# Layer 0's second projection in full fp32, attention ahead of the S5 products, and main products dealt by weight

## The chip, the cores and the metric

The kernel runs on one core of one Trainium2 chip. The metric is the device time of one execution in microseconds (us), the median of several runs. A core has a matrix engine (TensorE, PE in the profile, with its weight loads as PEld), a vector engine (VectorE, DVE), a scalar engine (ScalarE, ACT), a general one (GpSimd, POOL) and a queue that issues DMAs (SyncE, SP). Each engine works its own instructions in a fixed order, and waits for others by semaphores.

## The reference

Two layers of an encoder. Each layer normalizes its input, projects it, runs three mixers beside each other on parts of the projection (a gated linear recurrence with a convolution, an S5 state space model, sliding-window attention with rotary positions), projects their outputs back, and adds an MLP with squared ReLU:

```python
hn = _rms_norm(x, p['norm1'])
proj = hn @ p['w_in']
u_a, g_a, u_b = proj[..., :o1], proj[..., o1:o2], proj[..., o2:o3]
q = proj[..., o3:o4]; k = proj[..., o4:o5]; v = proj[..., o5:]
...
mix = jnp.concatenate([out_a, out_b, out_c], axis=-1) @ p['w_out']
x = x + mix
act = jnp.square(jax.nn.relu(_rms_norm(x, p['norm2']) @ p['w_up']))
x = x + act @ p['w_down']
```

The model width is 1024, the MLP's 4096, and there are 512 prompt and 128 sample frames. All inputs and outputs are fp32.

## The kernel before, in words

The 640 frames are cut into two groups g of 320 columns (256 prompt and 64 sample frames). Activations are kept transposed, with the width in 8 tiles of 128 partitions.

**Units and halves.** The work of PE is mostly weight products. A `Unit` is one block of 128 output columns over the 8 tiles of the width; it goes in two halves of 4 tiles each. A *split* unit has its weights cut in a high part wh (an ACT copy, L243) and a low part wl (a DVE subtraction, L244), activations likewise, and makes three products for each tile (L274, L275, L276). A *full* unit makes one fp32 product for each tile (L271) from weights as they come by DMA; the profile shows two records for each of these. Before the change only group 0 of layer 0's projection is full. `stream` is a generator that gives one half at a step and empties a unit's bank when it is done; there are three PSUM banks for units ("mm"), four for small products ("sm") and one for norms ("fin").

**Norm.** `Norm` scales the input by its gain only (L348 in a full one; L351 on ACT and L352 on DVE in a split one). The sum of squares goes through ACT, POOL and at last three one-column products on PE (L377); then eight small DVE operations (L396 to L403) make the reciprocal root, and PE spreads it over the partitions (L414). The result r scales what comes out of the banks. cs, the cosines and sines of the rotation times r, is scaled on POOL (L730). A k or q tile is copied by DVE as t = bank x cosine (L702 for k, L696 for q), by ACT as sw, which POOL multiplies by the sine (L693), and summed by DVE.

**Mixers.** `mixers` holds three generators: L (recurrence; its convolution is L760), S (S5: L832 makes the scans' inputs on PE, then scans on DVE, L850, with products on ACT, POOL and DVE, up to L855) and A (attention: loads, own keys, scores of the cached frames L963, probabilities, the transposes of their scaled scores L956 at L176, values L981, and then for each of 4 chunks of queries scores L1006, a turn by transposes with copies on ACT and DVE, L1020, and values L1027). The string TURNS says in which order they get a step. `weave` deals the halves of a stream evenly between the steps.

**Order.** PE's order is the code's order. On the other engines a scheduler decides it, with high priority for the emptying of full units' banks and for the norm. The S5 constants (`s5_const`) are made in the first 60 us by chains of complex products (L523 to L529), B's on DVE and C's on POOL, from values that DVE makes first (AR at L491); DVE makes other small constants in front of these (L439 to L518).

```python
    TURNS = "ALSSLSSSS" "LAAAAAA" + 5 * "SAA" + "A"
    ...
    weave(iter(()), 1, A, 15)
    weave(small, 2, A, 3)
    M = mixers(0, P, 0, q[0], m[0], setup[0])
    weave(M, 9, A, 4)
```

A is the stream of the projection, small the S5 constants' products, M the mixers.

## Time and profile before

| | before |
|---|---|
| runs, us | 1424.63, 1427.09, 1428.07 (median 1427.09) |
| profiled execution, us | 1423.95, span 1422.1 |
| TensorE's mean granted clock | 0.981 |
| PE, weight loads | 1358.9 us (96%), 1300.3 us (91%) |
| DVE, ACT, POOL | 876.0 us (62%), 651.7 us (46%), 359.4 us (25%) |

The profile is of one execution. Busy time is the time in which an engine worked on instructions; the rest of the span it waited or had nothing to do. The granted clock is 1.0 at 2.4 GHz and 0.5 at 1.2.

### The profile page before, as it was taken

What the parts mean: (1) busy time and instruction counts of PE and PEld (TensorE: products, weight loads), DVE (VectorE), ACT (ScalarE), POOL (GpSimd) and SP (SyncE); (2) the same over time, 40 slices, a digit from 0 to 9 for tenths busy, and PEclk for the clock granted to TensorE, in tenths of its full rate; (3) what the DMA queues carried; (4) which work ended last, traced back from release to release, by engine and by line L of the source; (5) the groups of instructions that cost most, each with busy time, mean ns of one, the idle gap of its engine ahead of it and who ended that gap; (6) DMA issues with size and microseconds to landing.
All of it is one profiled execution on the core that took longest, in us unless ns stands there. A gap on an engine that the chain in (4) does not pass through costs nothing.

```text
span 1422.1 us, 25428 instructions
## 1 busy us (share of the span) xinstructions
PE 1358.9 (96%) x9444; PEld 1300.3 (91%) x9444; DVE 876.0 (62%) x1726; ACT 651.7 (46%) x1347; POOL 359.4 (25%) x581
## 2 busy tenths in 40 slices
PE   7859979999999999999989998999999999999997
PEld 5648869899999999999988997999999999999997
DVE  7987696756554345356697769675654434435574
ACT  4365765545332132136675667554542212313543
POOL 5754364301042017001243325320101100100111
PEclk9979999999999999999999999999999999999998
DMA  7211332344422222234433332333442222223452
GB/s 261 81 61 63 116 104 101 125 151 145 151 72 78 74 75 63 81 120 149 143 99 112 120 126 83 112 112 126 142 149 89 75 75 75 75 75 117 151 177 91
DMA packets 91387, 156.24 MB, mean 110 GB/s; under 512 B 14336, under 2 KB 18304, under 8 KB 91264
## 3 DMA queue, kind: packets, MB, share of 16 engines
q1 hardware_dynamic: 91264, 154.63, 32.7%
q8 instruction: 74, 1.21, 0.3%
q14 instruction: 49, 0.40, 0.1%
HBM read 151.02 MB, written 3.37 MB: 109 GB/s over the span
## 4 chain that ended last, share of the span: by engine, by line
PE 82%; DVE 9%; POOL 4%; issue 2%; ACT 1%; DMA 0%; SPq 0%; DVEq 0%; ACTq 0%
PE mm L274 25%; PE mm L275 25%; PE mm L276 25%; PE sm L176 2%; DVE wl L244 1%; PE mm L271 1%; PE sm L1027 1%; DVE bigf L853 1%; DVE bigf L850 1%; PE sm L868 1%; PE fin L414 1%; PE sm L981 1%; PE sm L896 1%; PE sm L1006 1%; PE sm L832 0%
## 5 line engine op out<-in xcount | busy, mean ns | idle before, releaser
L274 PE MATMUL mm<-bigr,wh 128*128 128x320 f32 x2592 | 817.6, 315 | 2.1 <-POOL bigr L156 1.8
L276 PE MATMUL mm<-bigr,wl 128*128 128x320 f32 x2592 | 805.3, 311 | 12.7 <-DVE wl L244 12.7
L275 PE MATMUL mm<-bigr,wh 128*128 128x320 f32 x2592 | 804.7, 310 | 1.6 <-DVE bigr L1112 1.6
L243 ACT ACTIVATE wh<-raw 128x512 fp32r<-128x512 f32 x520 | 327.4, 631 | 504.9 <-PE mm L275 484.2
L274 PEld LDWEIGHTS mm<-bigr,wh 128*128 128x128 f32 x2592 | 490.2, 189 | 15.7 <-issue 5.8
L276 PEld LDWEIGHTS mm<-bigr,wl 128*128 128x128 f32 x2592 | 490.4, 189 | 14.0 <-DVE wl L244 14.0
L275 PEld LDWEIGHTS mm<-bigr,wh 128*128 128x128 f32 x2592 | 490.6, 189 | 3.0 <-DVE bigr L1112 2.1
L244 DVE TENSOR_TENSOR wl<-raw,wh 128x512 fp32r<-128x512 f32 x520 | 375.9, 724 | 181.2 <-ACT wh L243 169.5
L156 POOL TENSOR_SCALAR bigr<-t 128x320 fp32r<-128x320 f32 x128 | 63.3, 496 | 611.2 <-ACT t L1110 611.1
L1094 DVE TENSOR_TENSOR xT<-xT,mm 128x320 f32<-128x320 f32 x160 | 77.9, 487 | 135.4 <-PE mm L276 135.2
L1110 ACT ACTIVATE t<-t 128x320 f32<-128x320 f32 x128 | 60.0, 472 | 120.3 <-DVE t L1109 104.5
L1112 DVE TENSOR_TENSOR bigr<-t,bigr 128x320 fp32r<-128x320 f32 x128 | 71.0, 556 | 71.5 <-POOL bigr L156 71.2
L1109 DVE SCALAR_TENSOR_TENSOR t<-mm,r 128x320 f32<-128x320 f32 x128 | 62.1, 489 | 74.5 <-PE mm L276 73.7
L371 POOL TENSOR_TENSOR ss<-ss,sq 128x320 f32<-128x320 f32 x58 | 53.2, 918 | 201.4 <-ACT sq L364 194.6
L364 ACT ACTIVATE sq<-xT 128x320 f32<-128x320 f32 x66 | 30.6, 463 | 17.0 <-POOL ss L371 11.0
L271 PE MATMUL mm<-bigf,raw 128*128 128x320 f32 x104 | 31.8, 453 | 3.0 <-DVE t L702 2.4
L693 POOL TENSOR_TENSOR sw<-sw,cs 128x320 f32<-128x320 f32 x20 | 18.1, 905 | 58.2 <-ACT sw L692 44.4
L176 PE MATMUL sm<-ident,att 128*128 128x128 f32 x88 | 13.9, 289 | 19.7 <-DVE att L956 19.1
L956 POOL TENSOR_SCALAR att<-att,st 128x192 f32<-128x192 f32 (+2 forms) x24 | 22.6, 950 | 39.5 <-ACT wh L243 31.0
L351 ACT ACTIVATE bigr<-xT,sm 128x320 fp32r<-128x320 f32 x56 | 30.5, 560 | 2.7 <-DVE xT L1094 1.0
L271 PEld LDWEIGHTS mm<-bigf,raw 128*128 128x128 f32 x104 | 20.2, 199 | 11.9 <-DVE t L702 2.9
L352 DVE SCALAR_TENSOR_TENSOR bigr<-xT,sm,bigr 128x320 fp32r<-128x320 f32 x56 | 30.4, 551 | 0.1
(292 smaller groups left out, 1072.7 us busy)
## 6 DMA issues: line engine op xcount, KB each, us to landing
raw<-w_up SPq DMA_DIRECT2D x192, 256.0 KB, 2.6
raw<-w_down SPq DMA_DIRECT2D x192, 256.0 KB, 2.6
raw<-w_in SPq DMA_DIRECT2D x85, 256.0 KB, 2.6
raw<-w_out SPq DMA_DIRECT2D x64, 256.0 KB, 2.6
wl<-w_in SPq DMA_DIRECT2D x11, 256.0 KB, 4.0
xT<-x SPq DMA_DIRECT2D x8, 320.0 KB, 6.1
yT<-xT SPq DMA_DIRECT2D x8, 320.0 KB, 2.9
cs<-rope SPq DMA_DIRECT2D x4, 320.0 KB, 3.0
```

Source lines behind the costliest of these rows:

```text
L156: return G.tensor_scalar(out, in_, 1.0, 0.0, OP.mult, OP.add)
L243: act(h, raw, AF.Copy)
L244: tt(l, raw, h.bitcast(F32), OP.subtract)
L271: mm(pt, lhsT=self.w[n][:, k % 4], rhs=m[:, k], start=k == 0, stop=k == 7)
L274: mm(pt, lhsT=h[:, k % 4], rhs=m[:, k, 0], start=k == 0, stop=False)
L275: mm(pt, lhsT=h[:, k % 4], rhs=m[:, k, 1], start=False, stop=False)
L276: mm(pt, lhsT=l[:, k % 4], rhs=m[:, k, 0], start=False, stop=k == 7)
L371: G.tensor_tensor(self.ss, self.ss, sq, OP.add)
L1094: tt(xT[:, g, k], xT[:, g, k], pt, OP.add)
L1109: V.scalar_tensor_tensor(t, pt, 0.0, norm.r, OP.max, OP.mult)
L1110: act(t, t, AF.Square)
L1112: mark["dve"] = tt(am[:, f, 1], t, am[:, f, 0].bitcast(F32), OP.subtract)
```

## The change

Layer 0's projection is in full fp32 for group 1 as well, so its 24 halves take L271 on weights as loaded. In group 0 of layer 0 the squares of the norm are kept apart, and PE sums them in 24 one-column products (L395 of the new file) instead of POOL's additions and three products. That projection's units come in another order: k, v, q0 to q3, then ua, ub and ga. The first eight attention steps of this group come before the products of the S5 constants. `weave` gets a list of weights, one for each step: how many halves come behind it; TURNS holds both, with a list of its own for layer 0's group 0 (True). Projection, output projection and the first MLP piece are chained to one stream, so that the weights run over their borders. In the recurrence two copies of states move up, and one more step is cut. Tiles of the projection are allocated when first written.

```diff
-    def weave(steps, n, fill, m):
-
-        done = 0
-        for i in range(n):
+    def chain(*gens):
+        for g in gens:
+            yield from g
+
+    def later(f):
+        yield from f()
+
+    def weave(steps, weights, fill, m):
+
+        done, w, total = 0, 0, sum(weights)
+        for v in weights:
             next(steps, None)
-            while done < (i + 1) * m // n:
+            w += v
+            while done < int(w * m / total + 1e-6):
                 next(fill, None)
                 done += 1
...
             if full:
-                self.h = Carve(bigf()).at(0, 8, NG)
+                c = Carve(bigf())
+                self.h, self.sq = c.at(0, 8, NG), c.at(8 * NG, 8, NG)
...
-            if k == 0:
+            if self.full and self.g == 0:
+                act(self.sq[:, k], x, AF.Square)
+                if k == 0:
+                    V.tensor_scalar(self.sq[:, 0], self.sq[:, 0], 1e-6 * DM / 128, None, OP.add)
+                self.todo.append((self.sq[:, k], k == 0, k == 7))
+            elif k == 0:
...
+        order = (4, 5, 6, 7, 8, 9, 0, 1, 2, 3, 10, 11) if L == 0 and g == 0 else range(12)
...
-    TURNS = "ALSSLSSSS" "LAAAAAA" + 5 * "SAA" + "A"
+
+    TURNS = {False: "A0 L3 S1 S1 L1 S1 S1 L1 S2 S6 A1 A1 L6 A2 A1 A1 A1 A1 S2 A1 A1 S2 A1 A1 S3 A1 A1 S3 A1 A1 S2 A1 A1".split(),
+             True: "A1 A1 A1 A1 A1 A1 A1 A1 L4 A1 A1 L1 A1 S1 S1 L1 A1 A2 S1 S1 A1 A1 S2 S6 A1 L6 A1 A1 S2 S2 S2 S2 S2".split()}
+    WEIGHTS = {k: [int(t[1:]) for t in v] for k, v in TURNS.items()}
...
-        norms[g] = Norm(g, n1(0), full=g == 0)
+        norms[g] = Norm(g, n1(0), full=True)
...
-    weave(iter(()), 1, A, 2)
+    turns(A, 2)
     dma(sm[:, 80:], a["sm"][:, 80:])
     small_prep()
     s5_small(lru_const())
     small = layer_small(0, P)
     next(small)
     first(1)
-    weave(iter(()), 1, A, 15)
-    weave(small, 2, A, 3)
+    turns(A, 10)
     M = mixers(0, P, 0, q[0], m[0], setup[0])
-    weave(M, 9, A, 4)
-    run(A)
+    tw = WEIGHTS[True]
+    F = chain(A, stream(in_proj(0, 1, norms[1], q[1])))
+    weave(M, tw[0:9], F, 9)
+    run(small)
+    weave(M, tw[9:], F, 19)
+    tw = WEIGHTS[False]
     for L in range(DEPTH):
         last = L == DEPTH - 1
-        A = stream(in_proj(L, 1, norms[1], q[1]))
-        weave(M, 23 if L == 0 else 8, A, 16)
-        run(M)
+        if L:
+            F = stream(in_proj(L, 1, norms[1], q[1]))
+            turns(F, 10)
         M = mixers(L, P, 1, q[1], m[1])
-        weave(M, 9, A, 8)
-        run(A)
         hm = {}
-        F = stream(out_proj(L, 0, m[0], hm))
-        weave(M, 7, F, 16)
-        run(F)
-        F = stream(mlp(L, 0, (0,), hm, fresh=(0,)))
-        weave(M, 16, F, 28)
+        F = chain(F, stream(out_proj(L, 0, m[0], hm)), later(lambda: stream(mlp(L, 0, (0,), hm, fresh=(0,)))))
+        weave(M, tw, F, 58 if L else 52)
         run(M, F)
         run(stream(out_proj(L, 1, m[1], hm)))
...
-            A = stream(in_proj(L + 1, 0, norms[0], q[0]))
-            weave(iter(()), 1, A, 14)
+            F = stream(in_proj(L + 1, 0, norms[0], q[0]))
+            turns(F, 10)
             M = mixers(L + 1, P, 0, q[0], m[0])
-            weave(M, 9, A, 10)
-            run(A)
-            F = stream(mlp(L, 3, (1,), hm, nxt, norms))
-            weave(M, 15, F, 32)
-            run(F)
+            F = chain(F, stream(mlp(L, 3, (1,), hm, nxt, norms)))
+            weave(M, tw, F, 46)
+            run(M, F)
```

Three places show how instructions move. The first is PE's start, before and now, from the first unit on (L271 is a product of a full unit with weights in tiles raw or wl; L377 and L395 sum squares, L414 and L432 spread r, t is v's tile).

```order
L271 MATMUL mm<-bigf,raw 128x320 x12
L377 MATMUL fin<-ones,ss 128x1 x3
L271 MATMUL mm<-bigf,wl 128x320 x4
L271 MATMUL mm<-bigf,raw 128x320 x4
L414 MATMUL fin<-ident,rsq 128x128 x2
L414 MATMUL fin<-ident,rsq 128x64
L271 MATMUL mm<-bigf,wl 128x320 x4
L271 MATMUL mm<-bigf,raw 128x320 x4
```

```order
L271 MATMUL mm<-bigf,raw 128x320 x12
L395 MATMUL fin<-ones,bigf 128x1 x24
L271 MATMUL mm<-bigf,wl 128x320 x4
L271 MATMUL mm<-bigf,raw 128x320 x4
L432 MATMUL fin<-ident,rsq 128x128 x2
L432 MATMUL fin<-ident,rsq 128x64
L271 MATMUL mm<-bigf,wl 128x320 x4
L271 MATMUL mm<-bigf,raw 128x320 x4
L176 MATMUL sm<-ident,t 128x128 x2
```

Before, r is followed by units that are ua, ub and k; now the 12 and 8 products ahead of it and the one half behind it are k, v and q0, and the next is q1's.

The second is POOL's queue from group 1's squares (ss) to the first scaled tile sw, before up to the first product of the C constants (L524), now with lines moved by 18 or so (L542 to L547 are L524 to L529, L747 is L730, L710 is L693).

```order
L371 TENSOR_TENSOR ss<-ss,sq 128x320 x9
L660 TENSOR_TENSOR uap<-uap,r 128x256 x2
L661 TENSOR_TENSOR uap<-uap,r 128x4x16 x2
L730 TENSOR_TENSOR cs<-cs,r 128x320 x2
L371 TENSOR_TENSOR ss<-ss,sq 128x320
L156 TENSOR_SCALAR coll<-uap 128x3
L156 TENSOR_SCALAR uap<-sm 128x2x4x3
L156 TENSOR_SCALAR coll<-uap 128x3
L156 TENSOR_SCALAR coll<-uap 128x12 x2
L654 TENSOR_TENSOR ub<-ub,r 128x320
L524 TENSOR_TENSOR Cm<-s5s,tab 128x16x16
L528 TENSOR_TENSOR tab<-s5s,tab 128x256
```

```order
L389 TENSOR_TENSOR ss<-ss,sq 128x320 x6
L542 TENSOR_TENSOR Cm<-s5s,tab 128x16x16
L546 TENSOR_TENSOR tab<-s5s,tab 128x256
L541 TENSOR_TENSOR tab<-s5s,tab 128x256
L543 TENSOR_TENSOR Cm<-Cm,tab 128x16x16
L545 TENSOR_TENSOR tab<-s5s,tab 128x256
L542 TENSOR_TENSOR Cm<-s5s,Cm 128x16x16
L547 TENSOR_TENSOR tab<-tab 128x256
L541 TENSOR_TENSOR tab<-s5s,tab 128x256
L546 TENSOR_TENSOR tab<-s5s,tab 128x256
L747 TENSOR_TENSOR cs<-cs,r 128x320 x2
L543 TENSOR_TENSOR Cm<-Cm,tab 128x16x16
L710 TENSOR_TENSOR sw<-sw,cs 128x320
```

The scaling of cs stood ahead of all products of the C constants and stands behind nine of them.

The third is DVE's queue around the copy of turn 3 of group 0's attention (att from a bank of 128x512: L1020 before, L1037 now); L870 and L872 are scan steps (L853, L855 before), L776 is group 1's convolution (L760 before), L685 and L719 copies of ub and k.

```order
L956 TENSOR_SCALAR att<-att,st_1332 128x192 x2
L244 TENSOR_TENSOR wl<-raw,wh 128x512
L898 SCALAR_TENSOR_TENSOR bigf<-bigf 128x640
L1032 TENSOR_TENSOR bigr<-sm,bigr 128x4x64
L901 SCALAR_TENSOR_TENSOR bigr<-bigf,bigr 128x2x320
L244 TENSOR_TENSOR wl<-raw,wh 128x512
L1020 COPY att<-sm 128x512
L696 TENSOR_TENSOR t<-mm,cs 128x320
L697 TENSOR_TENSOR q<-t,sw 128x256
```

```order
L870 TENSOR_TENSOR bigf<-bigf,tab 128x640
L867 SCALAR_TENSOR_TENSOR bigf<-tab,bigf 128x640
L1049 TENSOR_TENSOR bigr<-sm,bigr 128x4x64
L872 TENSOR_TENSOR bigf<-bigf 128x640
L685 TENSOR_TENSOR ub<-mm,r 128x320
L870 TENSOR_TENSOR bigf<-bigf,tab 128x640
L776 SCALAR_TENSOR_TENSOR bigf<-uap,sm,bigf 128x332 x2
L872 TENSOR_TENSOR bigf<-bigf 128x640
L776 SCALAR_TENSOR_TENSOR bigf<-uap,sm,bigf 128x332 x4
L1037 COPY att<-sm 128x512
L719 TENSOR_TENSOR t<-mm,cs 128x320
```

The copy stood between weights' low halves and steps of S5's output, long behind the scans; now it stands directly behind both scans and the six steps of group 1's convolution.

## Rows read from the trace of the kernel before

**Rows 1.** The page's first part: busy us (share of the span) and instructions by engine.

```profile
PE 1358.9 (96%) x9444; PEld 1300.3 (91%) x9444; DVE 876.0 (62%) x1726; ACT 651.7 (46%) x1347; POOL 359.4 (25%) x581
```

**Rows 2.** Windows: length in us, busy us (count) of five engines, clock, DMA share, GB/s.

```profile
23.75:56.57 32.82, 29.14 (x104) 20.00 (x104) 32.17 (x108) 11.47 (x26) 23.94 (x36) 0.95 0.30 97
...
56.57:176.13 119.56, 101.35 (x746) 86.13 (x747) 91.28 (x208) 78.38 (x192) 56.35 (x90) 0.91 0.25 79
...
176.13:300.00 123.87, 113.38 (x848) 103.96 (x847) 94.41 (x176) 67.55 (x158) 53.17 (x73) 0.97 0.35 114
```

**Rows 3.** Waits of PE: us in total, times, longest us.

```profile
PE sm L176 <- DVE att L956: 19.1, 4, 10.4
...
PE mm L276 <- DVE wl L244: 12.7, 5, 4.1
```

**Rows 4.** Timeline of PE, 81 to 177 us: start, us, instruction, [idle before].

```profile
81.58 3.71 PE L832 MATMUL sm<-bigf,Bm 64*128 64x80 f32 x32 [6.16 <-DVE bigf L825]
...
105.91 0.66 PE L176 MATMUL sm<-ident,att 128*128 128x128 f32 x2 [10.37 <-DVE att L956]
...
176.13 0.56 PE L274 MATMUL mm<-bigr,wh 128*128 128x320 f32 x1
```

**Rows 5.** Timeline of PE in the later mixers: the attention's transposes.

```profile
205.43 0.78 PE L176 MATMUL sm<-ident,att 128*128 128x128 f32 x4 [3.45 <-DVE att L956]
...
748.25 0.86 PE L176 MATMUL sm<-ident,att 128*128 128x128 f32 x4 [1.03 <-DVE att L956]
...
890.03 1.09 PE L176 MATMUL sm<-ident,att 128*128 128x128 f32 x4 [4.23 <-DVE att L956]
```

**Rows 6.** Timeline of PE: halves of full units (eight records each).

```profile
27.01 2.32 PE L271 MATMUL mm<-bigf,raw 128*128 128x320 f32 x8
...
29.16 2.32 PE L271 MATMUL mm<-bigf,wl 128*128 128x320 f32 x8
...
46.81 3.96 PE L271 MATMUL mm<-bigf,raw 128*128 128x320 f32 x8 [2.42 <-DVE t L702]
...
85.21 3.54 PE L271 MATMUL mm<-bigf,wl 128*128 128x320 f32 x8
```

**Rows 7.** Windows: a stretch of split products alone.

```profile
450.00:500.00 50.00, 50.00 (x343) 50.00 (x342) 17.20 (x29) 8.86 (x14) 0.00 (x0) 1.00 0.22 75
```

**Rows 8.** The page's groups: making the low half; busy us, mean ns, idle before.

```profile
L244 DVE TENSOR_TENSOR wl<-raw,wh 128x512 fp32r<-128x512 f32 x520 | 375.9, 724 | 181.2 <-ACT wh L243 169.5
```

**Rows 9.** Timeline of DVE, 16 to 47 us.

```profile
16.35 0.55 DVE L352 SCALAR_TENSOR_TENSOR bigr<-xT,sm,bigr 128x320 fp32r<-128x320 f32 x1
...
32.31 0.19 DVE L491 TENSOR_TENSOR s5s<-bigf 128x32 f32<-128x32 f32 x1
...
36.69 1.13 DVE L524 TENSOR_TENSOR tab<-s5s,tab 128x256 f32<-128x256 f32 x1
...
38.86 1.03 DVE L760 SCALAR_TENSOR_TENSOR bigf<-uap,sm,bigf 128x332 f32<-128x332 f32 x2
...
42.89 0.41 DVE L524 TENSOR_TENSOR tab<-s5s,tab 128x256 f32<-128x256 f32 x1
...
46.28 0.48 DVE L702 TENSOR_TENSOR t<-mm,cs 128x320 f32<-128x320 f32 x1
```

**Rows 10.** One line's instructions on DVE: ns min/median/max, first and last start.

```profile
L348 DVE TENSOR_SCALAR bigf<-xT,sm x8: 374/382/977, 4.7 to 10.0; 128x320 f32<-128x320 f32 x8
```

**Rows 11.** Timeline of POOL, 27 to 49 us.

```profile
27.19 1.69 POOL L730 TENSOR_TENSOR cs<-cs,r 128x320 f32<-128x320 f32 x2
...
32.59 0.62 POOL L524 TENSOR_TENSOR Cm<-s5s,tab 128x256 f32<-128x256 f32 x1 [1.16 <-DVE s5s L491]
...
42.48 1.33 POOL L527 TENSOR_TENSOR tab<-s5s,tab 128x256 f32<-128x256 f32 x1
...
47.83 0.80 POOL L528 TENSOR_TENSOR tab<-s5s,tab 128x256 f32<-128x256 f32 x1
```

**Rows 12.** Timeline of DVE: the last step of group 0's scan chain.

```profile
103.63 0.81 DVE L855 TENSOR_TENSOR bigf<-bigf 128x640 f32<-128x640 f32 x1
```

More of the change, by code (lines that the diff above doesn't have):

```diff
@@ L323, in run, with turns @@
                 pass
-    def weave(steps, n, fill, m):
-        done = 0
-        for i in range(n):
+    def chain(*gens):
[6 more added lines that the diff above has]
+        for v in weights:
             next(steps, None)
-            while done < (i + 1) * m // n:
+            w += v
+            while done < int(w * m / total + 1e-6):
                 next(fill, None)
                 done += 1
+    def turns(fill, m):
+        for _ in range(m):
+            next(fill, None)
     class Norm:
@@ L638, in encoder_kernel, with in_alloc @@
         pass
-    def in_alloc(q):
-        q.uap = tp.tile([128, 2, 336], F32, tag="uap", name="uap", bufs=1)
-        q.ub = tp.tile([128, 2, NG], F32, tag="ub", name="ub", bufs=2)
-        q.q = tp.tile([128, 4, 256], F32, tag="q", name="q", bufs=2)
-        q.qS = tp.tile([128, 4, 4, 16], F32, tag="qS", name="qS", bufs=2)
-        q.ga = tp.tile([128, 2, NG], F32, tag="ga", name="ga", bufs=1)
-        q.kS = tp.tile([128, 64], F32, tag="kS", name="kS", bufs=1)
-        q.vS = tp.tile([128, 64], F32, tag="vS", name="vS", bufs=1)
+    def in_alloc(q, *names):
+        sh = {"uap": (2, 336), "ub": (2, NG), "q": (4, 256), "qS": (4, 4, 16), "ga": (2, NG), "kS": (64,), "vS": (64,)}
+        for n in names:
+            if not hasattr(q, n):
+                setattr(q, n, tp.tile([128, *sh[n]], F32, tag=n, name=n, bufs=2 if n in ("ub", "q", "qS") else 1))
     def in_evac(L, P, g, q, kind, i, pt):
         r = q.r
+        in_alloc(q, *{"ua": ("uap",), "k": ("kS",), "v": ("vS",), "q": ("q", "qS")}.get(kind, (kind,)))
         early = q.early[kind] if kind in q.early else 0
@@ L719, in begin @@
                 kvs[L] = {"kT": cst.tile([128, 512], F32, tag="kT", name="kT"), "vt": cst.tile([128, 4, 128], F32, tag="vt", name="vt")}
-            in_alloc(q)
             q.early = {"ua": 2, "ub": 2} if L == 0 and g == 0 else {"ua": 2}
@@ L737, in evac @@
             return f
-        items = [Unit(w_in[n], [(lambda: norm.h, evac(kind, i))], norm, norm.full, raws if n == 0 else None)
-                 for n, (kind, i) in enumerate(units)]
+        items = [Unit(w_in[n], [(lambda: norm.h, evac(*units[n]))], norm, norm.full, raws if n == order[0] else None) for n in order]
         items[1].mid, items[2].mid = norm.flush, factors
@@ L760, in lru @@
                 V.scalar_tensor_tensor(xc, u[:, ct, j:j + LP], col("conv_w", 8 * L + 2 * j + ct), xc, OP.mult, OP.add)
+            gcopy(P["coll"][:, ct, 9 + 12 * g:21 + 12 * g].rearrange("p (b t) -> p b t", t=3), us[:, ct, :, 16:19])
+            gcopy(P["coll"][:, ct, 33:36], u[:, ct, 256:259])
         for ct in range(2):
@@ L763, in lru @@
             yield
-            gcopy(P["coll"][:, ct, 9 + 12 * g:21 + 12 * g].rearrange("p (b t) -> p b t", t=3), us[:, ct, :, 16:19])
-            gcopy(P["coll"][:, ct, 33:36], u[:, ct, 256:259])
             for n, dst in enumerate((t_, i_)):
@@ L776, in lru @@
             act(t_, t_, AF.Tanh, scale=sp, bias=sp)
+        yield
         act(t2, t2, AF.Sqrt, scale=0.25)
@@ L903, in s5, with attention @@
             dma(o["send"][L], P["send"])
-    def attention(L, P, g, q, mix, c, cs):
+    def attention(L, P, g, q, mix, c, cs, o):
         c, mix = c(), mix()
@@ L913, in attention @@
         vn, pn = ([c.at(o, 2, 128)[h] for h in half] for o in (1792, 2048))
-        sets = [[cs.at(3200 + 640 * n, 2, 320) for n in range(2)], [c.at(640 * n, 2, 320) for n in range(2)]]
+        sets = [[cs.at(o + 640 * n, 2, 320) for n in range(2)], [c.at(640 * n, 2, 320) for n in range(2)]]
         PTs = [c.at(1280 + 512 * n, 2, 256) for n in range(2)]
@@ L923, in loads, with own @@
                 dma(vc[:, hf], a["vc"][L, 2 * g + hf])
+        def own():
             gcopy(kcT[:, :, :, 128:144], q.kS.rearrange("p (h b t) -> p h b t", t=16, h=2))
-        def own():
             b = bank3("sm", 4, 128)[0:16]
@@ L1084, in mixers @@
         G3 = {"L": lru(L, P, g, q, lambda: gens(0), c), "S": s5(L, P, g, q, lambda: gens(0), c),
-              "A": attention(L, P, g, q, lambda: gens(0), catt, c)}
-        for t in TURNS:
-            next(G3[t], None)
+              "A": attention(L, P, g, q, lambda: gens(0), catt, c, 3200 if scratch is None else 1280)}
+        for t in TURNS[scratch is not None]:
+            next(G3[t[0]], None)
             yield
@@ L1148, in first @@
             if g == 0 and k < 4:
-                raws.append(wload(a["w_in"][0, 0], k // 2))
+                raws.append(wload(a["w_in"][0, 4], k // 2))
         for k in range(8):
@@ L1208, in encoder_kernel @@
         F = stream(mlp(L, 1, (0, 1), hm))
-        weave(iter(()), 1, F, 16)
+        turns(F, 16)
         if not last:
@@ L1217, in encoder_kernel @@
         if not last:
-            weave(small, 2, F, 40)
+            weave(small, [1, 1], F, 40)
         run(F)
```

## The prediction

> **What bounds the kernel now.** I read the shares of the engines first. TensorE (PE) is busy for 1358.9 of 1422.1 us, VectorE (DVE) for 876.0 [rows 1], so all that an edit can win is PE's idle time, some 63 us, and all that it adds to PE's products is paid unless it falls into such idle time. Then the windows, which say where the idle time lies. From 23.75 to 56.57 us PE is busy for 29.14 of 32.82 us, from there to 176.13 (the first product of out_proj) for 101.35 of 119.56 at a mean clock of 0.91, and from there to 300 for 113.38 of 123.87 [rows 2]. The waits give the names: 19.1 us in four waits of the transposes at L176 for the attention's scaled scores (L956), and 12.7 us in five waits of a split product for the low half of its weight (L244) [rows 3]. The timeline places them: 10.37 us at 105.91 and 6.16 at 81.58 in layer 0's group 0 [rows 4], 3.45 at 205.43, 1.03 at 748.25 and 4.23 at 890.03 in the later mixers [rows 5]. Elsewhere PE runs without a gap, so DVE matters only where one of its chains lets PE wait.
>
> **Price of the fp32 units.** A half of a full unit comes every 2.15 us (27.01 to 29.16) [rows 6]. A split half is twelve products, and 343 of them fill 50 us [rows 7], so it takes 1.75. The 24 halves of group 1 cost 24 x 0.40 = 9.6 us more of PE. They give DVE 24 L244 of 0.724 us back [rows 8], 17 us, and ACT as many copies, but neither is what PE is short of on average; this counts only where a DVE chain is late. The 21 added one-column products for the squares run while PE would wait for the reciprocal root anyway, so I count nothing for them.
>
> **The start, up to the third q product.** PE has three banks for main products. Before, the first units were ua and ub, which ACT empties without any factor; k came fifth, and its copy (L702) stood at 46.28 on DVE [rows 9]. Now k, v and q0 fill the three banks, and q1, the seventh half, can't start until k is copied. On DVE the copy's place is still behind the S5 constants. What left the queue ahead of it: six L760 (two take 1.03, so 3.0 us) and the difference between eight L352 and eight L361, 0.55 less 0.38 each [rows 9, 10], 1.4 us; L368 goes out and group 1's L386 comes in at the same cost. So DVE is there at 46.28 - 4.4 = 41.9. The copy also needs cs, which POOL scaled at 27.19 [rows 11] and now scales behind nine products of the C constants. These can start when DVE has made AR (L491, 32.31 + 0.19 [rows 9], less 1.4 now: 31.1). The nine of before, from 32.59 to 47.83, took 0.62 to 1.34 us each [rows 11] and 7.9 in all, so they end at 39.0, and cs with its 1.69 at 40.7: before DVE's 41.9, by little. So DVE decides, the copy of 0.48 ends at 42.4, and PE goes on there.
>
> At this place DVE and POOL work side by side. In the rows POOL's product at 42.48 took 1.33 us, while DVE's own at 42.89, inside it, took its 0.41; at 36.69 DVE's took 1.13 for the same shape [rows 9, 11]. Which of the two pays changes from row to row; since eight of the nine products stood beside the same stretch of DVE's queue before, 14 us with what they cost it, I add nothing. The Trainium skill, "SBUF — State Buffer", section "SBUF: two separate sides", has it that a DVE operation with two SBUF inputs and a GpSimd operation that reads SBUF hold one port pair exclusively, whoever starts first, and the other is blocked for that whole instruction. The two rows agree with it, one on each side. It speaks against dealing both chains into the wait for k: if DVE lost on each of nine what it lost at 36.69, 0.72, the copy would come 6.5 later, and so would the sum; if POOL always lost (1.33 each, 12 us), cs would come at 44.8 and the sum would rise by 2.
>
> **From there to out_proj.** 42 full halves remain, 42 x 2.15 = 90.3 us. The small products are those of before: 119.56 - 18.2 idle (119.56 less 101.35) - 24 x 1.75 - 7 x 2.15 - about 5 lost to the clock leaves 39 us. (The clock's 5: PE ran at half speed for about 6 us behind 81.58 and 5 behind 105.91, as the full half of 85.21 shows with 3.54 for 2.32 [rows 4, 6].) I put 4 us for the clock now: a half took 3.96 after the wait that ended at 46.81 [rows 6], 1.6 too long, and there will be about one such half behind the wait for k and one or two behind turn 3. The old waits of 6.16 and 10.37 have no place in the new order: the attention's scores come before the scans, so the transposes no longer stand behind them. In their stead stands turn 3. Its copy (L1037) is queued on DVE behind both scans and behind group 1's six convolution steps (L776). Scan work ran from about 85.2, when its product was done (the next half starts at 85.21), to 104.44, when the last L855 was done [rows 6, 12], 19 us, and six convolution steps make 22. Between the first scan product and values(3) PE has seven full halves, 15 us, and some 2 us of small products, so it waits 5. Three more waits (the cached scores, their transposes, the gate's product) I put at 1 us each, the size of the wait at 748.25 [rows 5]. The sum is 42.4 + 90.3 + 39 + 8 + 4 = 183.7 against 176.13: **7.6 us later**. The bounds: no wait at turn 3 or beside it and none of the clock's 4, 7.6 - 12 = -4; DVE slowed on each of nine rows by the 0.72 of 36.69, and turn 3 twice as late, +19.
>
> **The later mixers.** The turns' weights put eight to ten halves between the cached scores and their transposes (after the scores' turn 1 half, then L6 and A2), where four or five stood (16 halves over 7 turns). A half gives PE 1.75 us of work and takes 0.72 of DVE's, so four more halves win DVE 4 x 1.03 = 4.1 us before PE asks. That is as much as the waits at 205.43, 748.25 and 890.03 [rows 5]: I count all three gone, 3.45 + 1.03 + 4.23 = **8.7 us**, and 1 us of halved clock behind the two long ones. The waits for L244 (12.7 us) I leave: they come within the scans, where DVE's order, not the number of halves behind it, lets PE starve; two scan products now stand two or three halves apart instead of one, but that spreads the burst less than its 10 us. The bounds: none gone, 0, and all of both kinds gone, -8.7 - 12.7 - 2 = -23.
>
> **Sum.** The profiled execution took 1423.95 us, 1.85 more than its span. 1423.95 + 7.6 - 8.7 - 1 = 1421.9. The median of the runs lies 3.1 above the profiled one, so I expect about **1425 us**, which nobody can tell from 1427.09: a measurement of this kernel tells about 0.3%, 4.3 us, from no change.
>
> **The rivals.**
> *Faster: the spacing also feeds the L244.* If the scans' products, now further apart, let the low halves through, the 12.7 us go with the others: 1425 - 12.7 = 1412. For it speaks that the L244 waits come only in the 10 us behind a scan product; against it that a scan step is as long as before and the order on DVE is still dense there. I give it 0.32.
> *Slower: turn 3 waits for POOL too.* Group 1's scaling of uap and cs now stands on POOL between the two scans' steps; cs takes 1.69 [rows 11], uap about as much again, 3.5 us in all, by which the second scan and the copy behind it come later. PE then waits 8.5 instead of 5, and runs at half clock behind that wait as it did behind 105.91, some 3 us more than I counted: 1425 + 6.5 = 1431.5. It decides if the copy L1037 ends over 26 us after PE's first scan product. For it speaks that the chain is a strict one, against it that DVE has the convolution to do in the meantime, which the sum counts behind the scans. 0.14.
> *Slower: the dealing brings nothing.* If the three waits stay, because DVE is late by more than the four halves give it, only the start's loss is left: 1425 + 9.7 = 1435. For it speaks that in the same mixers PE waits for DVE at L244 as well, 12.7 us in all, so the lateness at the transposes can be larger than the wait there shows. 0.18.
> *No change, as summed:* 0.36, with its own range of 1419 to 1431; about a quarter of it lies outside the 4.3 us, more of it below.
>
> **How the numbers follow.** Faster: 0.32 and 0.06 of the forecast, 0.38. Slower: 0.18, half of the 0.14 (1431.5 lies at the bound) and 0.03 of the forecast, 0.28. The rest, 0.34, is no change. The range has to reach both sides: from 1408, four below the faster rival, to 1439, four above the slower one of more weight; beyond it lie the far ends of the bounds at the start and in the mixers.
>
> **What would show it.** PE goes on with q1 at 41 to 45 us, k's copy (L719) right ahead of it and the second L747 done 1 to 2 us earlier; the first product of out_proj is at 181 to 187; a wait of 3 to 7 us at the products of values(3) (L1044) behind the copy L1037; no wait over 1 us at the cached scores' transposes behind 200 us; waits for L244 of 10 to 14 us in all. The prediction is wrong if out_proj starts before 177 or after 191, or if the L244 waits are gone.

## The result: slower by 1.1%

| | before | after |
|---|---|---|
| median of four runs each, us | 1425.86 | 1440.99 |
| all runs, us | 1423.15 to 1428.07 | 1438.52 to 1443.7 |
| ratio, 95% interval | | 1.0107 [1.0081, 1.0134] |
| profiled execution, span, us | 1423.95, 1422.1 | 1443.7, 1441.9 |

The forecast was 1425 (1408 to 1439). The time lies 2 us above the range, and the loss is far outside what a measurement can confuse with no change. The profiled execution of after is its slowest run, 2.7 us above the median, and the one of before is among its faster ones, so the two profiles differ by 19.8 us where the ratio says some 15. Before's own runs lie in two clusters (on the chip of the first experiments 1422.5 to 1425.2 and 1428.2 to 1429.6 us), so its median jumps with the cluster, and what follows goes by the ratios with their intervals.

The first part of the page after, against [rows 1]:

```profile
PE 1382.0 (96%) x9390; PEld 1299.8 (90%) x9390; DVE 856.9 (59%) x1702; ACT 631.5 (44%) x1315; POOL 357.8 (25%) x575
```

DVE lost 19 us of work, as reckoned. PE gained 23, where the fp32 halves were put at 9.6: 4.6 are the one-column sums (5.42 for 0.80), and for the rest its products ran longer than their number says, in part at a lower clock. Windows of after (columns as in [rows 2]): up to the seventh half, q1; to out_proj's first product; to the end; and layer 1's mixers.

```profile
0.00:41.01 41.01, 25.84 (x127) 20.03 (x127) 32.59 (x149) 13.90 (x31) 16.98 (x36) 0.86 0.58 208
41.01:190.28 149.27, 136.54 (x724) 94.59 (x725) 84.98 (x207) 68.83 (x175) 63.73 (x104) 0.95 0.26 83
190.28:1441.90 1251.62, 1219.63 (x8542) 1185.14 (x8540) 739.36 (x1348) 548.73 (x1110) 277.09 (x435) 0.99 0.32 108
703.42:1017.34 313.92, 299.27 (x2198) 277.53 (x2197) 230.71 (x443) 193.33 (x442) 98.17 (x137) 0.97 0.34 112
```

out_proj starts at 190.28 instead of 176.13 [rows 2], 14.15 later. The third row's stretch was this one in before:

```profile
176.13:1422.10 1245.97, 1211.96 (x8526) 1181.94 (x8524) 736.60 (x1349) 550.56 (x1104) 269.25 (x434) 0.99 0.33 109
```

That is another 5.65, of which about 1.1 is sixteen scan products that now stand behind out_proj's first product. So in this pair of profiles both parts lose, where the forecast had 7.6 lost at the start and 9.7 won behind it. But most of the 5.65 belongs to this one execution. Four kernels below with the same dealing and the same order from here on take 1247.4 to 1247.5 us for the stretch; the one with the S5 products first:

```profile
184.33:1431.80 1247.47, 1215.41 (x8542) 1181.93 (x8540) 739.51 (x1348) 548.35 (x1110) 276.67 (x435) 0.99 0.35 108
```

An estimate of what the clock cost, by windows of 6 us (length times what the granted clock lacks to 1), gives 18.5 us in after, 13.5 in this kernel and 15.3 in before. So the dealing itself loses about 1.5 us here, 1.1 of them the scan products, and the start is most of the loss.

The waits of PE, which answer to [rows 3]:

```profile
PE mm L276 <- DVE wl L244: 15.7, 13, 2.4
PE mm L271 <- issue: 10.7, 1, 10.7
PE sm L1044 <- ACT att L1035: 5.4, 1, 5.4
PE sm L1044 <- ACT att L963: 4.1, 1, 4.1
...
PE sm L998 <- DVE att L990: 2.1, 4, 0.9
```

The transposes' waits for DVE's scaled scores, 19.1 us before, are gone from this list. In their place stand others. The timeline of PE says where:

```profile
18.68 4.09 PE L271 MATMUL mm<-bigf,wl 128*128 128x320 f32 x8
...
41.01 4.60 PE L271 MATMUL mm<-bigf,raw 128*128 128x320 f32 x8 [10.73 <-issue]
...
110.95 1.04 PE L1044 MATMUL sm<-att,vt 128*64 128x256 f32 x4 [4.07 <-ACT att L963]
111.92 3.68 PE L271 MATMUL mm<-bigf,raw 128*128 128x320 f32 x8
...
143.13 1.98 PE L1044 MATMUL sm<-att,vt 128*64 128x256 f32 x8 [5.37 <-ACT att L1035]
145.04 4.18 PE L271 MATMUL mm<-bigf,raw 128*128 128x320 f32 x8
```

Each long wait is followed by products that take nearly twice their time (4.60, 3.68 and 4.18 for 2.32), so each costs another 1.3 to 2.3 us behind it. The wait of 10.73 is put down to "issue", since no engine's event lies right in front of it; DVE's timeline shows what PE waited for:

```profile
34.90 1.13 DVE L541 TENSOR_TENSOR tab<-s5s,tab 128x256 f32<-128x256 f32 x1
...
36.65 1.08 DVE L543 TENSOR_TENSOR tab<-tab 128x256 f32<-128x256 f32 x1
...
38.19 0.41 DVE L542 TENSOR_TENSOR tab<-s5s,tab 128x256 f32<-128x256 f32 x1
...
40.43 0.48 DVE L719 TENSOR_TENSOR t<-mm,cs 128x320 f32<-128x320 f32 x1
```

k's copy (L719) ends at 40.91 and q1 starts at 41.01. The copy is the last row of a dense queue of constants (tab, s5s). Its other input was ready long before, by POOL's timeline:

```profile
33.50 0.62 POOL L546 TENSOR_TENSOR tab<-s5s,tab 128x256 f32<-128x256 f32 x1
34.08 1.67 POOL L747 TENSOR_TENSOR cs<-cs,r 128x320 f32<-128x320 f32 x2
35.71 0.90 POOL L543 TENSOR_TENSOR Cm<-Cm,tab 128x256 f32<-128x256 f32 x1
36.57 0.88 POOL L710 TENSOR_TENSOR sw<-sw,cs 128x320 f32<-128x320 f32 x1
```

Behind turn 3 two copies end close together, DVE's (L1037) and ACT's (L1035), and PE goes on at 143.13, behind the later one:

```profile
142.05 0.68 DVE L1037 COPY att<-sm 128x512 f32<-128x512 f32 x1
142.48 0.60 ACT L1035 ACTIVATE att<-sm 128x512 f32<-128x512 f32 x1
```

### The profile page after: what moved, and what is told of

Read it like the earlier page. It is cut to its first block, busy times and chain, and to the rows that moved or that the text cites. A ratio compares the mean times of both kernels' runs of the same rounds, so it can differ in the third digit from the quotient of the medians.

```text
span 1441.9 us, 25210 instructions
## 1 busy us (share of the span) xinstructions
PE 1382.0 (96%) x9390; PEld 1299.8 (90%) x9390; DVE 856.9 (59%) x1702; ACT 631.5 (44%) x1315; POOL 357.8 (25%) x575
## 4 chain that ended last, share of the span: by engine, by line
PE 80%; DVE 6%; POOL 5%; ACT 3%; issue 2%; DVEq 0%; POOLq 0%; ACTq 0%
PE mm L274 24%; PE mm L276 23%; PE mm L275 23%; PE mm L271 3%; PE sm L176 1%; PE sm L1044 1%; DVE wl L244 1%; DVE bigf L867 1%; PE sm L1023 1%; PE sm L885 1%; PE sm L913 1%; PE fin L432 1%; ACT bigf L855 0%; PE fin L395 0%; PE sm L998 0%
## 5 line engine op out<-in xcount | busy, mean ns | idle before, releaser
L276 PE MATMUL mm<-bigr,wl 128*128 128x320 f32 x2496 | 777.2, 311 | 15.7 <-DVE wl L244 15.7
L274 PE MATMUL mm<-bigr,wh 128*128 128x320 f32 x2496 | 785.6, 315 | 2.4 <-POOL bigr L156 1.9
L275 PE MATMUL mm<-bigr,wh 128*128 128x320 f32 x2496 | 775.0, 310 | 1.7 <-DVE bigr L1132 1.6
L243 ACT ACTIVATE wh<-raw 128x512 fp32r<-128x512 f32 x496 | 311.8, 631 | 484.2 <-PE mm L275 467.7
L276 PEld LDWEIGHTS mm<-bigr,wl 128*128 128x128 f32 x2496 | 472.0, 189 | 20.7 <-DVE wl L244 20.4
L274 PEld LDWEIGHTS mm<-bigr,wh 128*128 128x128 f32 x2496 | 472.3, 189 | 13.8 <-issue 7.4
L275 PEld LDWEIGHTS mm<-bigr,wh 128*128 128x128 f32 x2496 | 472.6, 189 | 3.0 <-DVE bigr L1132 2.4
L244 DVE TENSOR_TENSOR wl<-raw,wh 128x512 fp32r<-128x512 f32 x496 | 352.9, 712 | 172.5 <-ACT wh L243 161.8
L271 PE MATMUL mm<-bigf,raw 128*128 128x320 f32 x200 | 63.9, 467 | 10.9 <-issue 10.7
L271 PEld LDWEIGHTS mm<-bigf,raw 128*128 128x128 f32 x200 | 39.7, 205 | 29.4 <-issue 16.1
L271 PE MATMUL mm<-bigf,wl 128*128 128x320 f32 x184 | 56.1, 449 | 0.0
L271 PEld LDWEIGHTS mm<-bigf,wl 128*128 128x128 f32 x184 | 35.0, 196 | 14.1 <-issue 1.9
L710 POOL TENSOR_TENSOR sw<-sw,cs 128x320 f32<-128x320 f32 x20 | 19.9, 997 | 55.3 <-ACT sw L709 48.0
```

The lines of the kernel that those rows point to most:

```text
L243: act(h, raw, AF.Copy)
L244: tt(l, raw, h.bitcast(F32), OP.subtract)
L271: mm(pt, lhsT=self.w[n][:, k % 4], rhs=m[:, k], start=k == 0, stop=k == 7)
L274: mm(pt, lhsT=h[:, k % 4], rhs=m[:, k, 0], start=k == 0, stop=False)
L275: mm(pt, lhsT=h[:, k % 4], rhs=m[:, k, 1], start=False, stop=False)
L276: mm(pt, lhsT=l[:, k % 4], rhs=m[:, k, 0], start=False, stop=k == 7)
```

## Experiments: which part costs

My theory after the result was that the start costs most of it, through chains on DVE, POOL and ACT that PE waits for, and the dealing little. The rivals were that the fp32 products themselves are the price (9.6 us of PE), or that the dealing is. Four kernels take one part each.

**Full fp32 alone** (before, with one line changed).

```diff
-        norms[g] = Norm(g, n1(0), full=g == 0)
+        norms[g] = Norm(g, n1(0), full=True)
```

> The kernel before, with group 1's projection in full fp32 and nothing else. Theory A (the fp32 halves are paid on TensorE in full): 24 x 0.40 = 9.6 us more, 1433 to 1436 us beside 1426. Rival B (what VectorE saves, 17 us of low halves, shortens the waits at the start and pays the halves back): 1426 or less.

Measured 1429.0 against 1428.2 on that chip, 1.0020 [1.0009, 1.0031], by the ratio some 3 us for 9.6 us of added products: between theory A and rival B. In the profile out_proj starts 5.58 later. The added work fell partly into idle time: the wait of 10.37 at the transposes [rows 4] is 9.36, and the one of 6.16 is 4.75.

```profile
78.48 3.43 PE L832 MATMUL sm<-bigf,Bm 64*128 64x80 f32 x32 [4.75 <-ACT bigf L776]
...
103.06 0.66 PE L176 MATMUL sm<-ident,att 128*128 128x128 f32 x2 [9.36 <-DVE att L956]
```

**Everything but the full fp32** (after, that line taken back).

```diff
-        norms[g] = Norm(g, n1(0), full=True)
+        norms[g] = Norm(g, n1(0), full=g == 0)
```

> The changed kernel, with group 1's projection split again. Theory A: 9.6 us come back, 1431 us beside 1441. Rival B (with the new order VectorE needs the relief): the low halves bring waits in, 1438 or more. Rival C (the start's new waits at k, at the first values and at turn 3 are the loss, not the halves): 1438 to 1444, since these waits stay.

Measured 1437.82, 1.0087 [1.0067, 1.0107]. PE has 9.6 us less to do, yet out_proj starts at 190.51, no earlier than after's 190.28. Turn 3's wait is 7.34 for 5.37, the gate's 2.80 for 0.93, and a new one of 1.74 comes up. The window from q1 on, against the second of after's above:

```profile
41.25:190.51 149.26, 132.16 (x820) 105.94 (x820) 100.36 (x235) 81.07 (x198) 67.22 (x105) 0.90 0.28 83
```

Of the 9.6 us, 4.4 became waiting (17.1 for 12.7), and 5 went into slower products: the clock is 0.90 for 0.95 in this execution, the slowest of six. DVE and ACT have their copies of the weights back, and their chains end no sooner. By the ratio some 3 us of the 15 are the fp32 products, with intervals that overlap.

**The old start with the new dealing** (after; first units, sums, group 1's split products and order up to out_proj as before; `even` is the old weave, OLD the old TURNS).

```diff
-            if self.full and self.g == 0:
+            if False:
...
-        order = (4, 5, 6, 7, 8, 9, 0, 1, 2, 3, 10, 11) if L == 0 and g == 0 else range(12)
+        order = range(12)
...
-    weave(M, tw[0:9], F, 9)
-    run(small)
-    weave(M, tw[9:], F, 19)
+    M = mixers(0, P, 0, q[0], m[0], setup[0], old=True)
+    even(M, 9, A, 4)
+    run(A)
+    F = stream(in_proj(0, 1, norms[1], q[1]))
+    even(M, 23, F, 16)
+    run(M)
```

> The changed kernel with the start of the one before: old unit order, sums on GpSimd, split group 1, attention behind the S5 products, even dealing up to the end of group 0's mixers; the new dealing by weight from group 1's mixers on. If the new dealing costs what the two traces differ by behind the first product of out_proj (5.6 us): 1431 us. If it pays what the prediction said (8.7 us and 1 of the clock): 1416. If it does nothing: 1426.

Measured 1426.26, 1.0001 [0.9987, 1.0016]: as fast as before. So the loss comes with the start. It equals the expectation for a dealing that does nothing. The waits of its PE say the same of the dealing as after's: the transposes' waits in the later mixers are gone (the one left is the start's 10.32), and L244's have grown from 12.7.

```profile
PE mm L276 <- DVE wl L244: 17.8, 13, 2.3
PE sm L176 <- DVE att L982: 10.3, 1, 10.3
PE sm L858 <- DVE bigf L851: 6.1, 1, 6.1
```

**The new start with the old dealing** (after; from group 1's mixers on the old turns, dealt evenly).

```diff
-        F = chain(F, stream(out_proj(L, 0, m[0], hm)), later(lambda: stream(mlp(L, 0, (0,), hm, fresh=(0,)))))
-        weave(M, tw, F, 58 if L else 52)
-        run(M, F)
+            even(M, 9, F, 8)
+            run(F)
+            F = stream(out_proj(L, 0, m[0], hm))
+            even(M, 7, F, 16)
...
```

> The changed kernel with the old even dealing and the old order of turns from group 1's mixers on; the start is the new one. If the dealing costs 5.6 us: 1435 us. If it does nothing: 1441. If it pays 8.7 us, as the prediction said, and the start alone lost more than seen: 1450.

Measured 1438.37, 1.0091 [1.0073, 1.0110]: the new start alone keeps most of the loss. Its windows behind out_proj's first product and over layer 1's mixers, beside the last two of after above:

```profile
190.74:1436.60 1245.86, 1212.43 (x8526) 1182.70 (x8524) 735.68 (x1346) 549.47 (x1102) 271.02 (x432) 0.99 0.34 109
703.41:1011.71 308.30, 293.89 (x2199) 274.88 (x2197) 229.67 (x443) 195.34 (x442) 95.31 (x137) 0.98 0.37 114
```

The same products in layer 1's mixers take 308.30 us under the old dealing and 313.92 under the new. PE is idle for 14.4 and 14.7 of them, so the difference is in busy time, 293.89 to 299.27. By the estimate over 6 us windows the clock costs 8.5 us under the new dealing, in after's execution, and 5.1 under the old, 3.4 of the 5.4; the rest of the busy time is not accounted for. The new dealing trades two or three long waits for many of up to 2.4 us, as many us in all. By the ratios it is worth between nothing (1.0001) and 2.3 us of loss (1.0107 less 1.0091, with intervals that overlap); it wins nothing.

## Experiments: what in the start

**The S5 products ahead of the attention again** (after).

```diff
-    weave(M, tw[0:9], F, 9)
     run(small)
+    weave(M, tw[0:9], F, 9)
```

> The changed kernel with the S5 constants' products ahead of the first attention steps again; the dealing and the rest stay. Were it the attention ahead of them that pushes VectorE's table work (which follows these products) into the first values' wait of 4.07 us: that wait goes, less what TensorE now waits at the constants themselves, 1436 to 1439 us. If the place of these products does nothing: 1441.

Measured 1436.03, 1.0068 [1.0045, 1.0090]: 5.6 us of the 15 come back (1.0107 less 1.0068; the intervals just overlap, so the size is rough), and out_proj starts at 184.33, 6 us earlier: 2.6 less waiting and 3.2 less busy time. The wait of 4.07 is 0.26, while turn 3 keeps its own:

```profile
107.25 0.65 PE L1044 MATMUL sm<-att,vt 128*64 128x256 f32 x4 [0.26 <-DVE bigf L842]
...
138.14 1.98 PE L1044 MATMUL sm<-att,vt 128*64 128x256 f32 x8 [5.73 <-ACT att L1035]
```

The expectations call the place of the 4.07 the first values. By the order on PE it is the second chunk's: the first products of L1044 come at 92.02 without a wait. The copies that they read (L1035, L1037 behind turn 1) had ended by 105.26; the releaser, L963, is the softmax of the next scores, which holds two of the four small banks. So PE most likely waits for a bank here.

DVE shows why the softmax is late. In after the late S5 products bring their DVE work (L620 to L630, tables of powers) into the stretch in which the steps ahead of it (L787, L688, L957, L961) are due:

```profile
100.10 1.52 DVE L621 TENSOR_TENSOR tab<-tab 128x496 f32<-128x496 f32 x1
101.55 1.34 DVE L787 SCALAR_TENSOR_TENSOR bigf<-bigf 128x332 f32<-128x332 f32 x1
102.81 1.71 DVE L622 TENSOR_TENSOR tab<-tab 128x496 f32<-128x496 f32 x1
104.44 0.48 DVE L688 TENSOR_TENSOR t<-mm,r 128x320 f32<-128x320 f32 x1
...
109.72 0.15 DVE L961 SCALAR_TENSOR_TENSOR st<-st,nskp 128x4 f32<-128x4 f32 x1
```

With the products ahead, the same rows come earlier, and nothing of L620 to L630 lies between them:

```profile
99.09 0.50 DVE L787 SCALAR_TENSOR_TENSOR bigf<-bigf 128x332 f32<-128x332 f32 x1 [2.18 <-ACT bigf L786]
100.68 0.49 DVE L688 TENSOR_TENSOR t<-mm,r 128x320 f32<-128x320 f32 x1 [1.08 <-PE mm L271]
...
106.64 0.15 DVE L961 SCALAR_TENSOR_TENSOR st<-st,nskp 128x4 f32<-128x4 f32 x1
```

**k's copy ahead of the B constants on DVE** (after; the constants are issued when k is done).

```diff
-    next(small)
     first(1)
-    turns(A, 10)
+    turns(A, 3)
+    with tc.issue_after(kmark["k"].ins):
+        next(small)
+    turns(A, 7)
```

> The changed kernel, in which the B constants' products on VectorE may start only behind k's copy (they stand ahead of it in the changed kernel), so that the 10.73 us wait for the bank of k shrinks to about 4. Theory D (the start ends by the sum on TensorE: products plus its waits): out_proj starts some 6 us earlier, 1434 to 1436 us beside 1441. Rival E (a chain of VectorE, GpSimd and ScalarE through the S5 constants, the scans and the attention ends the start, and TensorE only waits elsewhere): the 6 us come back as later waits, 1439 to 1443.

Measured 1439.09 against 1426.76, 1.0086 [1.0063, 1.0108], as rival E had it. The wait for k shrinks to 7.14, not to 4; q1 comes at 38.03, three us earlier, and PE pays them back at the scores of the cached frames, 3.91 for 0.87:

```profile
38.03 4.11 PE L271 MATMUL mm<-bigf,raw 128*128 128x320 f32 x8 [7.14 <-issue]
59.64 2.19 PE L981 MATMUL sm<-att,qS 64*64 64x144 f32 x16 [3.91 <-issue]
```

**The old sums on POOL** (after; no one-column products for group 0's squares).

```diff
-            if self.full and self.g == 0:
+            if False:
```

> The changed kernel with the squares of group 0's first norm summed on GpSimd again, and 3 one-column products instead of 24 (5.05 us in the trace). As the prediction had it, they lie in the wait for the reciprocal root and for k's copy: 1440 to 1442 us. If they delay anything: 1436 or less.

Measured 1438.1, 1.0079 [1.0055, 1.0104]. That is below the 1440 expected if the sums cost nothing, and above the 1436 if they delay something. On POOL the additions stand ahead of the C constants, and the scheduler puts k's copy at 29.12, ahead of most of DVE's. q1 starts 11 us earlier, and the same scores wait 10.30 for 0.87:

```profile
29.71 3.78 PE L271 MATMUL mm<-bigf,raw 128*128 128x320 f32 x8 [2.64 <-ACT sq L382]
...
57.37 2.19 PE L980 MATMUL sm<-att,qS 64*64 64x144 f32 x16 [10.30 <-POOL tab L156]
```

The POOL copy that the row names ended at 57.21. Later still ended DVE's copy of the last q (L716), at 57.27, behind B's products:

```profile
57.05 0.22 DVE L716 TENSOR_TENSOR qS<-t,sw 128x64 f32<-128x64 f32 x1
```

In after, here, with k first and in the next kernel these scores start 0.1 us behind the last L716. So an earlier k wins only what the last q's copy wins: 0.8 us with k first and 3.1 here, and out_proj comes 0.1 and 2.3 us earlier.

**All rotations ahead of all S5 constants** (k first as above, and the constants' rest is issued behind POOL's last rotation).

```diff
-    run(small)
+    with tc.issue_after(kmark["sw"].ins):
+        run(small)
```

> The changed kernel with both constants' chains behind the rotations: B's products on VectorE behind k's copy, C's products on GpSimd behind the last q's rotation. Theory E in a narrower form (GpSimd's queue, in which the rotations stand between the C products, sets when the first attention scores can run, at 60 us, and all behind them): these scores come some 8 us earlier and out_proj with them, 1432 to 1435 us beside 1441. Theory F (the S5 path behind the constants sets it): the wait moves to the S5 products, 1438 to 1444.

Measured 1435.62 against 1428.14, 1.0055 [1.0033, 1.0077]. This is just above theory E's range, and by the ratio the best of the kernels that move one piece of the start. The wait for k is 3.40, q1 comes at 34.02, and the scores wait 1.76, more than after's 0.87 but far less than 3.91 and 10.30; they come 7.0 us earlier than in after, and out_proj 6.2 (184.06). The waits of 4.08 and 5.36 behind them stand untouched.

```profile
34.02 3.31 PE L271 MATMUL mm<-bigf,raw 128*128 128x320 f32 x8 [3.40 <-issue]
53.43 1.20 PE L981 MATMUL sm<-att,qS 64*64 64x144 f32 x16 [1.76 <-POOL Cm L542]
...
104.92 1.12 PE L1045 MATMUL sm<-att,vt 128*64 128x256 f32 x4 [4.08 <-ACT att L964]
```

**The two units of ua first again** (after).

```diff
-        order = (4, 5, 6, 7, 8, 9, 0, 1, 2, 3, 10, 11) if L == 0 and g == 0 else range(12)
+        order = (0, 1, 4, 5, 6, 7, 8, 9, 2, 3, 10, 11) if L == 0 and g == 0 else range(12)
...
-    turns(A, 10)
+    turns(A, 16)
```

> The changed kernel with the two units ua ahead of k, whose banks ScalarE empties without waiting for anything: TensorE then has four more halves to do, 8.6 us, while k's copy is awaited, and the attention's first steps come four halves later in the order. Theory D: 1432 to 1435 us beside 1441. Rival E: 1438 to 1443, with more waiting at the first values or at turn 3.

Measured 1443.25, 1.0110 [1.0084, 1.0135]: no gain. The wait for k is 6.46 instead of 10.73, but it comes at 45.37, since ua's halves lie ahead of it, and turn 3 still waits 3.51 and 2.04. It is nearest to rival E, just above its 1443.

## Experiments: do the parts add

**S5 first and the old dealing** (the edits of both together).

> The changed kernel with two of its parts undone: the S5 constants' products ahead of the attention again, and the even dealing from group 1's mixers on. If the two losses add (5 us and 3 us in the runs so far): 1432 to 1434 us. If they overlap: 1436.

Measured 1434.16 against 1428.14, 1.0060 [1.0036, 1.0083]. Added ratios would give 1.0052, an overlap 1.0068; this can't be told from either. **The same with group 1 split again:**

> The same with group 1 split again; what is left of the change is the order k, v, q ahead of ua and ub, the sums on TensorE, and the weights in group 0's mixers. If the split gives back what full fp32 cost alone (1 to 3 us): 1430 to 1432 us. If at this place TensorE's products matter (9.6 us): 1424. If they don't, since the chains end the start: 1433.

Measured 1435.13, 1.0066 [1.0041, 1.0091]. PE has 9.6 us less to do and nothing of it shows in the time: turn 3 waits 8.65 for 5.75, the gate 2.82 for 0.93; out_proj starts at 184.92 for 187.44, and the stretch behind it takes 2.1 us longer (1247.98 for 1245.86).

**S5 first, the old dealing and k first:**

> The run with S5 products first and even dealing later (1434), and in it B's products on VectorE behind k's copy. There the saved wait for k went into a wait of the attention's scores for GpSimd; here the S5 products (3 us of TensorE) stand between. If the start is a sum: 4 us earlier, 1430 to 1431. If GpSimd's rotations still hold the scores: 1433 to 1436.

Measured 1438.92 against 1428.04, 1.0074 [1.0057, 1.0091]: above both expectations. The wait for k shrinks by 3.8 us and q1 comes at 38.18, 3 us earlier, and the S5 products, which need the constants behind it, now wait 3.31 at 57.28. **S5 first, the old dealing and ua first:**

> The run with S5 products first and even dealing later (1434), and in it the units ua ahead of k, so that TensorE has 8.6 us of halves in the wait for k; left of the change are full fp32 in group 1, the sums on TensorE and the weights of group 0's mixers. If the unit order was the rest of the loss: 1427 to 1430, as full fp32 alone. If not: 1432 to 1436.

Measured 1440.52, 1.0092 [1.0074, 1.0110], above both expectations and no better than without ua first (1.0060, the intervals just overlap). **The same with group 1 split and the sums on POOL,** so that of the start little but its turns' order and weights stays new:

> The same with group 1 split and the sums on GpSimd again; left of the change are the weights of group 0's mixers, q ahead of ub, and the small edits of the recurrence. If these are neutral: 1425 to 1428. If the weights of this mixer cost by themselves: 1430 or more.

Measured 1434.31, 1.0049 [1.0034, 1.0065]: 7 us, near half of after's loss, are still there. With full fp32, the sums, the late S5 products, the new dealing and most of the unit order undone, what is left is group 0's turns with their weights, and q ahead of ub; the small edits of the recurrence stand in the old start as well, which is level with before. The profile has out_proj at 179.68, 3.6 us later than before, and 6.6 more behind it, where two waits of the transposes make 11.9 us for 8.7 in three. **And from the other side, before with weights in group 0's mixers:**

```diff
-        weave(M, 23 if L == 0 else 8, A, 16)
+        if L == 0:
+            for n in [2, 1, 1, 5, 1, 1, 1, 1, 0, 0, 1, 1, 0, 1, 0, 1, 1, 0, 1, 1, 0, 0, 0]:
+                next(M, None)
+                for _ in range(n):
+                    next(A, None)
...
```

> The kernel before, and only the dealing of group 0's attention by weight: 5 halves between the first scores and the transposes of the cached ones, where one stood (the wait of 10.37 us), 20 halves in these turns instead of 16, fewer behind them. Theory D (a sum): the wait shrinks by 8 us, 1417 to 1420 us beside 1426. Theory E (the chain ends the start): TensorE waits later instead, 1424 to 1428.

Measured 1430.97, 1.0033 [1.0019, 1.0046], slower than either theory had it: these weights alone cost the kernel before some 5 us. The wait of 10.37 at the transposes [rows 4] is gone, and group 1's norm, whose DVE chain is now what PE reaches first, waits longer than that:

```profile
113.17 1.84 PE L414 MATMUL fin<-ident,rsq 128*128 128x128 f32 x6 [11.07 <-DVE rsq L403]
```

No version was faster than the kernel before; the new dealing on the old start equals it.

## Why the prediction was wrong

**What held.** k decides when PE goes on: q1 at 41.01, put at 42.4, behind L719 on DVE. cs was put at 40.7 and was done at 35.75. Most of that is an early start: AR was ready at 27.34, put at 31.1,

```profile
27.15 0.19 DVE L509 TENSOR_TENSOR s5s<-bigf 128x32 f32<-128x32 f32 x1
```

and 1.2 us come from POOL's short times (0.62 to 0.90). DVE paid beside POOL (0.8 to 1.13, and 0.41 from 37.85 on). The Trainium skill, "SBUF — State Buffer", section "SBUF: two separate sides", has a DVE operation with two SBUF inputs and a GpSimd operation that reads SBUF take one port pair exclusively; these rows agree, with DVE as the loser. That k's copy came so close to its 41.9 is in part luck: AR came 3.8 us earlier than reckoned, and DVE's stretch from there to the copy took 2.3 longer (13.1 us for 10.8). (If POOL had always lost, the sum would have risen by 2.9, not by 2.)

Turn 3's wait is 5.37, put at 5, and the chain that was named gives 5.0: DVE's copy ended at 142.73, PE's work ahead at 137.76. ACT's copy, which the prediction left out, added the rest. Here too two errors cancel: from the end of the first scan product, at 118.1, the chain took 24.6 us to the end of the copy, and PE's work ahead of it 19.6, where 22 and 17 were put. The transposes' waits in the later mixers are gone. Of the other signs, out_proj at 190.28 is behind the 181 to 187 expected, and the 15.7 us at L244 are above the 10 to 14.

**The step that failed most: "I count all three gone, 8.7 us".** The three waits did go. But the sum took a wait that goes for time that is won, and left L244's 12.7 us as they were. They became 15.7 in thirteen, four waits at L998 (2.1) and others came up, and from out_proj's first product on PE's idle time fell only from 34.0 to 32.0 us (1245.97 less 1211.96, 1251.62 less 1219.63), while its busy time rose by 7.7: 1.1 are the scan products, 3.2 the clock, by the estimate above, and the rest is not accounted for. The old start with the new dealing measures what the step is worth: nothing (1.0001). It is the rival "the dealing brings nothing", put at 1435 and 0.18, that came nearest, though not by its reason: the three waits did not stay.

**The second: the start's 7.6 us.** It cost 14.15 in the profile, and by the ratios about 15 (1.0107 against 1.0001 with the old start). By the terms of the sum: q1 came 1.4 earlier; the 42 halves are the 90.3; the waits are 12.7 (0.87, 0.31, 1.17, 4.07, 5.37, 0.93), put at 8; the clock behind them took 6.6 (4.60 for 2.32, 1.04 and 3.68 for 0.65 and 2.42, 1.98 and 4.18 for 1.09 and 2.42, where the second number is an undisturbed row's), put at 4; 39.7 are left for small products, put at 39. That makes 149.3 from 41.01. The largest single miss is the wait of 4.07 at the second chunk's values, which I did not have: I followed the chain to turn 3, and not what the S5 products bring to DVE when they come late. With the S5 products first that wait goes, and out_proj comes 6 us earlier. The one-column sums, counted at nothing, may have a price too: with POOL's sums the ratio is 0.0028 lower, 4 us, but the intervals overlap, and the rotations and k's copy move there too.

**Why the start costs that much although PE has only 9.6 us more.** The waits show chains through DVE, ACT and POOL at its end: constants, rotations, scans, the attention's turns. Added alone, the fp32 products cost 3 us of their 9.6; taken out of the new order, they give back 3 (1.0107 to 1.0087, with intervals that overlap) or nothing (1.0060 to 1.0066). What costs is the order, which sets the constants against k's copy and the rotations, and against the second chunk's values. By the ratios, the S5 products put first give 5.6 us for the latter (1.0107 to 1.0068), and all rotations put first 7.4 for the former (1.0107 to 1.0055, with intervals apart), while k alone or the sums alone shift much of the wait to the scores. No run makes both moves. And 7 us stand in the kernel that keeps little but group 0's turns and weights (1.0049), which the prediction gave no price of their own.

**Open.** The undoings don't add: S5 first gives 5.6 us and k first 3, and with the old dealing both together stand at 1.0074 where S5 first alone stands at 1.0060, though most of these intervals overlap. Chains were named for about half of the start's loss; the turns and weights of group 0 hold some 7 us, but which chain of theirs costs it, and what q ahead of ub does, can't be read from kernels in which every piece moves the others' waits. Nor is it settled why the clock was lower in after's profiled execution.

## What to carry to other kernels

In a stretch in which PE waits for chains of other engines, PE's own work says little of the price or the gain: here 9.6 us more cost 3, and 9.6 less gave back 3 or nothing. Follow the chain that ends next behind the wait that you remove, and count only what is left after that one (here L244 behind the transposes, the last q's copy behind k's, the norm behind the transposes). Before work is moved later, list what it issues on the other engines, and see whose chain is due there.

## What the runs showed of the hardware that I had not expected

After 24 one-column sums in a row (48 records, 5.4 us of PE without a gap) the next half took 4.09 us at 18.68, where the same half behind three such sums took 2.40 before; the granted clock of that stretch (18.68 to 22.61) is 0.57. PE was busy by the profile all the time before it fell. The slow half stands behind these sums in all eleven kernels here that have them, with 3.88 to 4.61 us; in nine of them the sums themselves already take 6.6 to 8.2.

The same wait may or may not be followed by a lower clock. With the S5 products first PE waits 2.73 us at 70.96, and with the old dealing as well 2.74 at 70.69, in the same order of work. The half behind takes 2.32 in the one and 4.01 in the other. The windows from 68 to 80 us, of the one:

```profile
68.00:80.00 12.00, 8.80 (x74) 5.52 (x73) 9.62 (x28) 4.48 (x20) 11.20 (x22) 1.00 0.12 44
```

and of the other:

```profile
68.00:80.00 12.00, 8.84 (x54) 5.67 (x55) 9.01 (x28) 4.32 (x19) 11.10 (x21) 0.86 0.13 44
```

PE is busy for as long with 54 products as with 74. Such a difference can lie in any comparison of two profiles here, so single profiles that differ by 2 us prove little.
